# Stick-breaking attention, RG-LRU and squared-ReLU MLP on one core: value products in plain fp32 on the two halves of the array, one plan for the MLP and the front, a finer opening, aligned buffers

## The chip, the cores and the metric

The kernel runs on one core of one Trainium2 chip. The metric is the device time of one execution in microseconds (us), taken as the median of several runs. The core has five engines with their own instruction queues: PE (matmuls; its weight loads are listed apart as PEld), DVE, ACT, POOL, and SP, which here only issues DMAs. Everything is computed to fp32 accuracy.

## What is computed

One transformer-like block on x of 1024 tokens by 1024 channels; only the shapes and the products matter here:

```python
def hybrid_mixer(h, ...):                       # h = rms_norm(x): 1024 x 1024
    proj = h @ w_in                             # q, k, v of 512 each, xl and gl of 512 each
    q, k = rms_norm per head of 64              # 8 heads
    attn = stick_breaking_attention(q, k, v)    # per block of 128 queries:
        #   z = q k^T / 8 ; log_w = log_sigmoid(z) + suffix sums of log_sigmoid(-z)
        #   w = exp(log_w) below the diagonal, else 0 ; out = w @ v
    lru = rg_lru(conv(xl)) * gelu(gl)
    return concatenate([attn, lru]) @ w_out

x = x + hybrid_mixer(rms_norm(x))
x = x + square(relu(rms_norm(x) @ w_up)) @ w_down     # 1024 -> 4096 -> 1024
```

## The kernel before

**Precision.** A large product is made of three matmuls. Each operand is split into a high half (a copy that rounds to the type fp32r, made by ACT) and a low half (the source minus the high half, a two-input subtraction on DVE or POOL). PE then runs low by high, high by low and high by high into the same PSUM bank. A matmul of this kind has a 128x128 stationary operand and a moving operand of up to 512 columns. Operands of type plain F32 can be multiplied too, without a split.

**The front.** Everything up to the second norm is called the front. `record_front` writes it down as operations with an engine, a cost, the tiles read and the tiles written. `Plan.schedule` then makes a list schedule of these operations. The order in which units are considered is the table `ORDER`; `BIAS` shifts the due time of each kind of operation; `ALT` lists by number, unit by unit, which operations go to their other allowed engine (DVE instead of POOL and the like). Every instruction is issued in the order that the plan gives, so that in a trace all of the front carries the helper's line, L927.

- Opening: `iunit` (L481) loads, for eight channel chunks kc, a transposed piece of x (256 KB) and a piece of w_in (128 KB) alternately. ACT and DVE make `hTh` and `hTl` (128x512 halves of x) and the halves of `wq` (128x256). `chain` (L510) is the product of a weight column block with x: four steps of two chunks (six matmuls) each, so a step waits until two chunks are ready.
- `qunit`, `gunit`: queries, keys and their norms. `ss` is a plain fp32 product, four stationary operands of 128x32 next to each other in the array. `lunit`: the recurrent part; its `pg` is a plain fp32 product with a 64-row operand in each half of the rows.
- `vunit` (L583): values. ACT writes the high half, DVE the low half, so a head's stationary operand is 128 columns wide: 64 high and 64 low.
- `aunit` (L677): for a head pair p and a block c of 256 queries, scores `z`, sigmoids, scans, weights w. Then for every m from c down to 0 (256 keys) and each head h of the two, PE transposes four (or three, at m = c) 128x128 blocks of w into `pw`, ACT copies the high half to `wt`, DVE writes the low half, and PE runs four matmuls (two key blocks by high and low) of 128x256 into head h's half of `av`. At m = c one key block has only 128 columns. The high rows of `av` then hold the product of the high values, the other 64 rows that of the low values; ACT copies one out (`ot`) and DVE adds the other (`ob`), for each head. There are 80 such (p, c, m, h) groups.
- `ounit` (po): the product with w_out. `hunit` (ht): transposes of the result for the MLP.

**The MLP.** After the front's plan comes code that is written in a fixed order (line L1056 in traces). Two groups g of 2048 hidden channels are each computed with fewer, summed products in the manner of Strassen. A product is 12 matmuls of 128x512. A group has seven phases: 16, 24 and 16 products up (`p` in traces), then 16 (da, db), 16 (ea, eb), 16 (ga, gc) and 8 (ha) down (banks `pa`, `pb`, `pc`); 224 products in all. The sums of weights are POOL's or DVE's, the products' results in `U` are made by ACT, DVE and POOL, the high halves by ACT, and nearly all low halves by DVE (`split2`, L1068). The loop at L1354 runs the products in order and prepares the stationary operand of product q + 6 and the moving operand of q + 4 behind product q. Tiles come from rings of two pools each: 2 + 6 raw tiles, 2 + 4 stationary tiles, 8 + 4 moving tiles. The first number lies in pools on the left side of the memory, the second in pools on the right side. In each partition the left pools' tiles of the kernel before begin at a multiple of 256 bytes, the right pools' tiles 224 bytes above one.

Of the kernel before, what the change touches and what calls it, by code (L numbers as in the profile page):

```python
# [60 lines left out]

BIAS = {"vec": -30, "": 12, "x": 5, "hTh": -22, "hTl": 14, "wq": 5, "whq": -19, "wlq": 23, "ssx": 23, "wo": 15, "woh": -25, "wol": -18,
        "wv": 30, "whv": 4, "wlv": -30, "bd": -3, "pq": 19, "sq": 21, "qkl": 6, "pk": 8, "kf": -14, "ssq": -9, "sse": -22, "sst": 3,
        "var": 11, "pow": 17, "exp": 18, "rb": 15, "nrm": 1, "nrq": 17, "pv": 22, "vl": -16, "w_up": -13, "sth": -16, "stl": -19, "rsb": 14,
# [43 lines left out]
class Plan:  # L108
    def __init__(self):
        self.ops, self.queue, self.unit = [], {}, 0  # L110
        self.inunit, self.uname, self.flex = 0, "", []
        self.groups = {}

# [3 lines left out]
    def op(self, eng, cost, fn, r=(), w=(), set=None, grp=None, kb=0, what="", work=None, port=None, alt=None):  # L117
        o = Op()
        self.inunit += 1
# [81 lines left out]
    def schedule(self):  # L201
        free = {e: 0.0 for e in KEEP}
# [38 lines left out]
        while len(done) < n:  # L241
# [98 lines left out]
            for k in o.closes:  # L340
                left[k] -= 1
                late[k] = max(late[k], o.end)
                if not left[k]:
                    if not k:
                        q = self.queue["u"]
                        a = nxt["u"]
                        nxt["u"] = min(len(q), a + COUNT["uu"])
                        for i in range(a, nxt["u"]):
                            alloc(q[i], f"uu{i - a}", late[k] + 50)
                    for tag in OPENS[k]:  # L350
# [17 lines left out]
def record_front(plan, E, order):  # L368
# [75 lines left out]
    def xload(kc, ch):  # L444
        o = slice(512 * ch, 512 * ch + 512)
        xt = plan.tile("lg", f"xt{kc}{ch}")
        op("SP", 0, lambda kc=kc, xt=xt: E.sp.dma_start(xt[:, 0:512], E.xt[kc * P:(kc + 1) * P, o]), w=[xt], kb=256, what=f"x{kc}{ch}")
# [33 lines left out]
    def iunit():  # L481
        for kc in range(KC):
            xload(kc, 0)
            wload("q0", kc)
# [414 lines left out]
def kernel(ctx, tc, x, xt, vecs, w_in, w_rg, w_ig, w_out, w_up, w_down, out):  # L899
# [75 lines left out]
    for t in PTAGS:  # L975
        spools[t] = pool(psums, f"f_{t}", space=PSUM)
# [434 lines left out]
```

## Time and profile before

| | |
|---|---|
| median of 3 runs | 1107.29 us (1105.79 to 1111.71) |
| profiled execution | 1107.23 us, of which the span is 1105.3 us and 1.9 us lie around it |
| mean granted PE clock | 0.997 |
| DMA traffic | 120.82 MB, mean 109 GB/s |
| instructions | 15275, of them 5368 matmuls |

Times inside the profile count from the start of the span. A row of a group names line, engine, operation, output <- inputs, shapes and count, then the busy time and the mean ns of one, then the idle time of the engine just before these instructions and who ended it. A row of the timeline has start, duration, engine and form. The end of a matmul is modelled: matmuls overlap, so the time that one takes in a dense run is the distance between starts.

### The profile page before, as it was taken

What the parts mean: (1) busy time and instruction counts of PE and PEld (TensorE: products, weight loads), DVE (VectorE), ACT (ScalarE), POOL (GpSimd) and SP (SyncE); (2) the same over time, 40 slices, a digit from 0 to 9 for tenths busy, and PEclk for the clock granted to TensorE, in tenths of its full rate; (3) what the DMA queues carried; (4) which work ended last, traced back from release to release, by engine and by line L of the source; (5) the groups of instructions that cost most, each with busy time, mean ns of one, the idle gap of its engine ahead of it and who ended that gap; (6) DMA issues with size and microseconds to landing.
All of it is one profiled execution on the core that took longest, in us unless ns stands there. A gap on an engine that the chain in (4) does not pass through costs nothing.

```text
span 1105.3 us, 15275 instructions
## 1 busy us (share of the span) xinstructions
PE 1080.4 (98%) x5368; PEld 879.7 (80%) x5368; DVE 841.0 (76%) x1172; ACT 629.9 (57%) x1150; POOL 408.2 (37%) x340
## 2 busy tenths in 40 slices
PE   7999999999998999999999999999999999999998
PEld 5987778988777788777888888778887888888786
DVE  7498688848986886568557789987568676989964
ACT  7678689739986774446227843434554257543441
POOL 2420233022134211113443658734024425668431
PEclk9999999999999999999999999999999999999999
DMA  9311202111119101233333235555433332245654
GB/s 305 125 44 45 62 5 68 44 44 40 39 44 346 58 29 49 67 107 113 124 114 96 67 96 169 175 151 160 145 97 133 124 95 77 90 143 168 209 159 146
DMA packets 80636, 120.82 MB, mean 109 GB/s; under 512 B 9136, under 2 KB 29104, under 8 KB 80560
## 3 DMA queue, kind: packets, MB, share of 16 engines
q1 hardware_dynamic: 78256, 115.66, 33.3%
q10 hardware_dynamic: 2304, 4.20, 1.0%
q8 instruction: 42, 0.69, 0.3%
q14 instruction: 34, 0.28, 0.1%
HBM read 107.77 MB, written 12.06 MB: 108 GB/s over the span
## 4 chain that ended last, share of the span: by engine, by line
PE 85%; DVE 7%; ACT 4%; DMA 2%; issue 1%; SPq 0%; POOL 0%; DVEq 0%; ACTq 0%
PE p L1056 26%; PE pa L1056 16%; PE pb L1056 8%; PE po L927 7%; PE pq L927 5%; PE pv L927 4%; PE pc L1056 4%; PE pxl L927 3%; PE pgl L927 3%; PE av L927 3%; PE z L927 2%; PE pw L927 2%; DMA x<-in_xt_dram 1%; ACT x L927 1%; DVE h L927 1%
## 5 line engine op out<-in xcount | busy, mean ns | idle before, releaser
L1056 DVE TENSOR_TENSOR U<-p,U 128x512 f32<-128x512 f32 x80 | 55.1, 689 | 65.8 <-PE p L1056 65.7
L927 PE MATMUL pq<-hTh,wq 128*128 128x512 f32 x256 | 86.5, 404 | 8.0 <-DVE wq L927 6.4
L1056 PE MATMUL p<-m0t,st 128*128 128x512 f32 x384 | 92.0, 399 | 2.3 <-DVE U L1056 2.3
L1056 POOL TENSOR_TENSOR U<-U 128x512 f32<-128x512 f32 x48 | 68.1, 1426 | 67.5 <-ACT U L1056 32.9
L1056 PE MATMUL p<-m1t,st 128*128 128x512 f32 x384 | 90.1, 393 | 1.2 <-DVE U L1056 1.2
L1056 PEld LDWEIGHTS p<-m0t,st 128*128 128x128 f32 x384 | 73.1, 191 | 19.9 <-issue 2.7
L1056 PEld LDWEIGHTS p<-m1t,st 128*128 128x128 f32 x384 | 72.0, 188 | 18.0 <-ACT sb L1056 1.6
L927 DVE TENSOR_TENSOR wt<-pw,wt 128x512 fp32r<-128x512 f32 (+1 forms) x80 | 50.3, 629 | 26.9 <-ACT wt L927 26.5
L1056 PE MATMUL p<-m0b,sb 128*128 128x512 f32 x288 | 68.3, 394 | 1.7 <-DVE nrs L1347 1.7
L1056 PE MATMUL p<-m1b,sb 128*128 128x512 f32 x288 | 68.0, 393 | 0.0
L1056 POOL TENSOR_TENSOR r_sb<-r_sb,r_sa 128x512 f32<-128x512 f32 x16 | 22.9, 1429 | 116.4 <-DMA r_sb<-in_w_up_dram 55.2
L1056 PEld LDWEIGHTS p<-m0b,sb 128*128 128x128 f32 x288 | 53.9, 188 | 14.5 <-issue 1.9
L927 PEld LDWEIGHTS pq<-hTh,wq 128*128 128x128 f32 x256 | 49.2, 192 | 20.3 <-DVE wq L927 8.0
L1056 PEld LDWEIGHTS p<-m1b,sb 128*128 128x128 f32 x288 | 54.0, 188 | 12.5
L927 ACT CAST wt<-pw 128x512 fp32r<-128x512 f32 (+1 forms) x80 | 43.5, 543 | 35.9 <-PE pw L927 33.1
L927 POOL TENSOR_TENSOR w<-w,G 128x1024 f32<-128x1024 f32 (+3 forms) x18 | 31.4, 1747 | 87.0 <-ACT w L927 54.4
L1056 ACT ACTIVATE U<-U 128x512 f32<-128x512 f32 x96 | 58.9, 630 | 6.0 <-DVE U L1056 2.8
L927 ACT ACTIVATE G<-z,qv 128x512 f32<-128x512 f32 (+3 forms) x96 | 51.3, 586 | 14.1 <-PE z L927 8.7
L927 PE MATMUL av<-wt,v 128*128 128x256 f32 (+1 forms) x320 | 54.5, 295 | 3.3 <-DVE wt L927 2.4
L927 DVE TENSOR_TENSOR_SCAN G<-G,K 128x257 f32<-128x257 f32 (+3 forms) x32 | 48.3, 1531 | 9.6 <-ACT G L927 9.5
L927 PE MATMUL pq<-hTl,wq 128*128 128x512 f32 x128 | 50.9, 398 | 0.0
L927 ACT ACTIVATE w<-z,qv 128x512 f32<-128x512 f32 (+3 forms) x96 | 50.7, 604 | 0.1
(240 smaller groups left out, 2930.4 us busy)
## 6 DMA issues: line engine op xcount, KB each, us to landing
ro<-in_w_out_dram SPq DMA_DIRECT2D x20, 256.0 KB, 4.7
x<-in_xt_dram SPq DMA_DIRECT2D x16, 256.0 KB, 4.7
x<-in_x_dram SPq DMA_DIRECT2D x8, 512.0 KB, 5.6
wrl<-in_w_in_dram SPq DMA_DIRECT2D x32, 128.0 KB, 2.4
x<-in_x_dram SPq DMA_DIRECT2D x16, 256.0 KB, 5.7
r_a<-in_w_up_dram SPq DMA_DIRECT2D x16, 256.0 KB, 2.9
r_b<-in_w_up_dram SPq DMA_DIRECT2D x16, 256.0 KB, 2.8
r_sa<-in_w_up_dram SPq DMA_DIRECT2D x16, 256.0 KB, 3.3
```

The costliest lines, as they stand in the source:

```text
L927: self.last = tc.keep_in_program_order(getattr(self.eng, op)(*args, **kw))
L1056: ins = getattr(self.eng, op)(*args, **kw)
```

## The change

1. **Value products.** The values stay F32 (one copy, 64 columns per head) and so does `wt`: one copy per `pw` tile, allowed on ACT or DVE, and put on DVE for all 80 by `ALT`. Head h of a pair uses columns 64h to 64h + 63 of the array and writes partitions 64h to 64h + 63 of one `av` tile, the heads alternating. Two m's share one step on PE where there are two, so the 80 groups become 24. `ot` is gone; `ob` is one copy, or, where the result is used directly, nothing at all. PE has 160 matmuls in place of 320, in plain fp32.
2. **One plan.** `record_mlp` writes the MLP down as operations too, and the plan schedules front and MLP together. The low halves, sums and squares may go to POOL or DVE as `ALT` says. In all, POOL makes 179 of the MLP's low halves (3 before), and 38 of its weight sums (128 before). By the plan's units POOL has 12 to 18 two-input instructions in a phase of 16 products (15 and 14 in ea, eb of the first and second group), 35 and 28 in the phase of 24, and 15 in that of 8; DVE has 13 to 50 two-input instructions without PSUM in a phase of 16 (49 and 50 in ea, eb), 29 and 36 in that of 24, 15 and 9 in that of 8. The matmuls of neighbouring products, and of the last transposes of the front, may be interleaved. The stores of the sums `r2` move from ACT's queue to SP's (16 DMAs).
3. **Opening.** `chain` for the first weights goes in steps of one chunk (three matmuls), and `iunit` records the weight ahead of x.
4. **Alignment.** Pads (`align`, `falign`, K1 1056, lg 544) put the left pools' tiles at a multiple of 256 bytes and the right pools' tiles 128 bytes above one.

`ORDER`, `BIAS` and `ALT` are new tables throughout; the counts of tiles change with them (`A` 4 to 2, `wr` 7 to 3, `w` 9 to 16, `ob` 1 to 2).

DVE in the opening, before. `hTl` is the low half of a piece of x, `wq` that of a piece of w_in, the t_ and sp_ tiles are constants:

```order
L927 TENSOR_TENSOR hTl<-x_83,hTh 128x512
L927 SCALAR_TENSOR_TENSOR wq_196<-x_83,vec,wq_196 128x256
L927 TENSOR_SCALAR sp__104<-sp__104,t_c 128x4
L927 TENSOR_TENSOR hTl<-x_83,hTh 128x512
L927 SCALAR_TENSOR_TENSOR wq_205<-x_83,vec,wq_205 128x256
L927 TENSOR_TENSOR hTl<-x_83,hTh 128x512
L927 SCALAR_TENSOR_TENSOR wq_213<-x_83,vec,wq_213 128x256
```

The same place now:

```order
L1205 TENSOR_TENSOR hTl<-x_90,hTh 128x512 x4
L1205 SCALAR_TENSOR_TENSOR wq_205<-x_90,vec,wq_205 128x256
L1205 SCALAR_TENSOR_TENSOR wq_208<-x_90,vec,wq_208 128x256
L1205 SCALAR_TENSOR_TENSOR wq_212<-x_90,vec,wq_212 128x256
L1205 SCALAR_TENSOR_TENSOR wq_216<-x_90,vec,wq_216 128x256
L1205 SCALAR_TENSOR_TENSOR wq_219<-x_90,vec,wq_219 128x256
L1205 SCALAR_TENSOR_TENSOR wq_231<-x_90,vec,wq_231 128x256
L1205 TENSOR_TENSOR hTl<-x_90,hTh 128x512
L1205 SCALAR_TENSOR_TENSOR gcol<-vec 128x1
```

The first weight's low half now stands behind four pieces of x, and the weights follow each other. On SP five pieces of x and the small vectors are issued before the first piece of w_in, where x and w_in alternated before.

PE at a value product of the first pairs, before. `pw` are transposes of the weights w, `av` the value product, `pxl` a product of the recurrent part that fills in between:

```order
L927 MATMUL pxl_1130<-hTh,wl_875 128x512
L927 MATMUL pw_1152<-ident,w_946 128x128
L927 MATMUL pw_1152<-ident,w_964 128x128
L927 MATMUL pw_1152<-ident,w_946 128x128
L927 MATMUL pw_1152<-ident,w_964 128x128
L927 MATMUL av_1023<-wt_1137,v_734 128x256 x4
L927 MATMUL pxl_1130<-hTh,wl_879 128x512
```

The same engine now, where block c = 2 begins (`pg` is the recurrent part's gate product):

```order
L1205 MATMUL pg_1362<-x_90,bd 128x512
L1205 MATMUL pg_1363<-x_90,bd 128x512
L1205 MATMUL pw_1370<-ident,w_1296 128x128
L1205 MATMUL pw_1370<-ident,w_1308 128x128
L1205 MATMUL pw_1370<-ident,w_1296 128x128
L1205 MATMUL pw_1370<-ident,w_1308 128x128
L1205 MATMUL av_1376<-wt_1274,v_699 64x256 x2
L1205 MATMUL av_1376<-wt_1274,v_699 64x128 x2
L1205 MATMUL av_1376<-wt_1354,v_1035 64x256 x4
L1205 MATMUL pxl_1388<-hTh,wl_886 128x512
```

One step now holds both heads and two m's: eight fp32 matmuls on halves, in place of four groups of four on the whole width between other work.

PE where the front ends, before. `ht` are the last transposes, `p` the first products of the MLP:

```order
L927 MATMUL ht_5121<-ident,x_83 128x128 x8
L927 MATMUL ht_5131<-ident,x_83 128x128 x8
L927 MATMUL ht_5143<-ident,x_83 128x128 x8
L927 MATMUL ht_5155<-ident,x_83 128x128 x8
L1056 MATMUL p_00_5246<-m0b_4941,sb_4963 128x512 x3
L1056 MATMUL p_00_5246<-m0b_4949,sb_4963 128x512 x3
```

The same place now:

```order
L1205 MATMUL ht_4745<-ident,x_90 128x128 x8
L1205 MATMUL ht_4756<-ident,x_90 128x128 x8
L1205 MATMUL p_00_4776<-m0b_4645,sb_4603 128x512 x3
L1205 MATMUL ht_4799<-ident,x_90 128x128 x8
L1205 MATMUL ht_4815<-ident,x_90 128x128 x8
L1205 MATMUL p_00_4776<-m0b_4652,sb_4603 128x512 x3
```

Three matmuls of the MLP's first product now stand between the second and the third group of transposes.

The diff, cut to its core:

```diff
-SHAPE = dict(... wt=([2, 512], F32R), ob=([256], F32), ot=([256], F32), lg=([516], F32),
-             ... v=([4, 4, P], F32R), ... av=([2, 256], F32),
+SHAPE = dict(... wt=([2, 512], F32), ob=([256], F32), lg=([544], F32),
+             ... v=([4, 4, HD], F32), ... av=([256], F32),
+             ... bk=([512], F32), U=([8, 4, 512], F32))
+MORE = {2: (("mv", 4), ("st", 4), ("ra", 6)), 4: (("bk", 4),)}
...
+       "m71": (1, 2, 4, 6,), "m72": (4, 5, 6,), "m73": (1,), "m74": (4, 5, 6,), "m75": (1, 3,), "m76": (4, 5, 8, 10,), "m77": (1, 3, 5,), "m78": (4, 8,),
...
     def iunit():
         for kc in range(KC):
-            xload(kc, 0)
-            wload("q0", kc)
+            wload("q0", kc, "i")
+            xload(kc, 0, "i")
...
     def chain(pd, key, col, ch, name):
-        for g in range(4):
+        step = 1 if key == "q0" else 2
+        for g in range(0, KC, step):
             def mm(g=g):
-                for kc in (2 * g, 2 * g + 1):
+                for kc in range(g, g + step):
...
-            op("ACT", 482, lambda i=i, t=t, src=src: E.act.mul(vv[:, i, :, 0:HD], src(), E.rstd1[:, t:t + 1]),
-            op("DVE", 474, lambda i=i, t=t, src=src: E.dve.scalar_tensor_tensor(vv[:, i, :, HD:P], src(), E.rstd1[:, t:t + 1],
+            op("ACT", 482, ev, r=[pd, (rstd1, t // 2)], w=[(vv, i)], what=f"vh{pp}{t}", alt=("DVE", 430, False))
...
+        for g in range(c, -1, -2):
+            ms = [m for m in (g, g - 1) if m >= 0]
...
+                    def ev(e, ww=ww, pw=pw, nw=nw, h=h):
+                        (E.act.copy if e == "ACT" else E.dve.tensor_copy)(ww[:, h, :nw], pw[:, :nw])
...
-                        for x in (1, 0):
-                            E.pe.matmul(av[:, h, q0:256], VV[p // 2, t // 4][:, t % 4, 2 * (p % 2) + h, :], ww[:, x, 256 * jj:256 * jj + 256 - q0],
+                        for h in range(2):
+                            E.pe.matmul(av[HD * h:HD * h + HD, q0:256], VV[p // 2, t // 4][:, t % 4, 2 * (p % 2) + h, :], ww[:, h, 256 * jj:256 * jj + 256 - q0],
...
-            op("ACT", 367, lambda ot=ot, h=h, hs=hs, os=os: E.act.copy(ot[hs], av[os, h]), r=[(av, h)], w=[ot], what=f"ot{p}{c}")
-            op("DVE", 420, lambda ot=ot, h=h, hs=hs: E.dve.tensor_tensor(ob[hs], av[hs, h], ot[hs], op=ALU.add), r=[(av, h), ot], w=[(ob, h)], what=f"ob{p}{c}")
+        op("ACT", 380, lambda e: (E.act.copy if e == "ACT" else E.dve.tensor_copy)(ob[:], av[:]), r=[av], w=[ob], what=f"ob{p}{c}", alt=("DVE", 420, False))
...
+def record_mlp(plan, E, base):
...
+    def split(tag, name, src, what):
+        v = plan.tile(tag, name)
+        op("ACT", 626, lambda: E.act.copy(v[:, 0], src[1]()), r=[src[0]], w=[(v, 0)], what=f"{what}h")
+
+        def low(e):
+            on(e).tensor_tensor(v[:, 1], src[1](), v[:, 0].bitcast(F32), op=ALU.subtract)
+        op("DVE", 687, low, r=[src[0], (v, 0)], w=[(v, 1)], what=f"{what}l", port=True, alt=("POOL", 1285, True))
+        return v
...
+            if store:
+                R2[g, k] = V(plan, None, f"r2{g}{k}")
+                op("SP", 0, lambda: E.sp.dma_start(E.r2[g][k], raw[:]), r=[raw], w=[R2[g, k]], kb=256, what="rst")
...
+    pool(ctx, "align", side="right").tile([P, 24], F32, name="align")
...
-                return lgs[:, 516 * v.slot:516 * v.slot + 516]
+                return lgs[:, 544 * v.slot:544 * v.slot + 544]
...
     record_front(plan, E, ORDER)
+    record_mlp(plan, E, len(ORDER))
     plan.schedule()
```

More of the change, by code (lines that the diff above doesn't have):

```diff
@@ L349, in schedule @@
                             alloc(q[i], f"uu{i - a}", late[k] + 50)
+                    for tag, more in MORE.get(k, ()):
+                        q = self.queue.get(tag, [])
+                        b = min(COUNT[tag], len(q))
+                        nxt[tag] = max(nxt.get(tag, 0), b)
+                        for i in range(nxt[tag], min(len(q), nxt[tag] + more)):
+                            alloc(q[i], COUNT[tag] + i - nxt[tag], late[k] + 50)
+                        nxt[tag] = min(len(q), nxt[tag] + more)
                     for tag in OPENS[k]:
@@ L518, in mm @@
                     E.pe.matmul(pd[:], w[:, 0, s], E.hTh[:, kc, m], start=False, stop=kc == KC - 1)
-            r = [(hT, (x, kc, ch)) for x in "hl" for kc in (2 * g, 2 * g + 1)]
-            op("PE", 6 * 228, mm, r=r + [W[key][2 * g][0], W[key][2 * g + 1][0]], w=[pd], what=name)
+            r = [(hT, (x, kc, ch)) for x in "hl" for kc in range(g, g + step)]
+            op("PE", 3 * step * 228, mm, r=r + [W[key][kc][0] for kc in range(g, g + step)], w=[pd], what=("i" if step == 1 else "") + name)
     SQ, RQ = {}, {}
@@ L945 @@
     nc.vector.memset(E.mhalf, -0.5)
-    E.rs2, E.w_out = rs2, w_out
+    E.rs2, E.w_out, E.w_down, E.out = rs2, w_out, w_down, out
+    E.nrs2 = const.tile([P, NT], F32, name="nrs2")
+    E.r2 = [dram.tile([8, P, 512], F32, name=f"r2_{g}") for g in range(2)]
     psums, left, right, late = ExitStack(), ExitStack(), ExitStack(), ExitStack()
@@ L973 @@
     nc.vector.memset(E.K1[:, 512:513], 1.0)
-    for t in PTAGS:
-        spools[t] = pool(psums, f"f_{t}", space=PSUM)
+    psz = ExitStack()
+    spools["z"] = pool(psz, "f_z", space=PSUM, side="left")
+    for t in CLOSES[3]:
+        spools[t] = pool(psums, f"f_{t}", space=PSUM, side="right")
     for t in CLOSES[1]:
@@ L979, with openu @@
     spools["wr"] = pool(right, "f_wr", side="right")
-    class Ring:
-        def __init__(self, na, nb):
-            self.na, self.n, self.i, self.pools = na, na + nb, 0, [None, None]
-        def tile(self, shape, dtype, **kw):
-            self.i += 1
-            return self.pools[(self.i - 1) % self.n >= self.na].tile(shape, dtype, **kw)
-    rwr, stp, mvp = Ring(2, 6), Ring(2, 4), Ring(8, 4)
-    rings = {"ra": (rwr, "r", 2), "st": (stp, "t", 2), "mv": (mvp, "t", 8)}
+    def openu():
+        if "U" not in spools:
+            late.close()
+            spools["U"] = pool(ctx, "units", side="right")
+            for t, _ in MORE[2]:
+                spools[f"{t}_"] = pool(ctx, f"{t}_", side="right")
     class Maker(Plan):
@@ L1005, in make @@
                     left.close()
-                    spools["h2"] = pool(ctx, "h2")
-                    for t, (ring, _, n) in rings.items():
-                        ring.pools[0] = pool(ctx, t, bufs=n)
-                if v.tag in rings:
-                    return rings[v.tag][0].tile([P] + shape, dt, tag=rings[v.tag][1], name=v.name)
+                    for t in OPENS[1]:
+                        spools[t] = pool(ctx, t)
+                if v.slot >= COUNT[v.tag]:
+                    openu()
+                    return spools[f"{v.tag}_"].tile([P] + shape, dt, tag=slot, name=v.name)
+            if v.tag == "U":
+                openu()
+            if v.tag == "bk":
+                k = v.slot >= COUNT["bk"]
+                if ("bk", k) not in spools:
+                    (psz if k else psums).close()
+                    spools["bk", k] = pool(ctx, f"bk{int(k)}", space=PSUM, side="left" if k else "right")
+                return spools["bk", k].tile([P] + shape, dt, tag=slot, name=v.name)
             if v.tag == "x1":
@@ L1330, in moving @@
-    def moving(n):
-        nonlocal free
-        if n < len(PR) and PR[n].mov is not None:
-            PR[n].item.add()
-            PR[n].mov()
-            free += PR[n].free
-    for k in ("0b11", "0b21"):
-        movs[k] = {u: (E.first[k, u][:, 0], E.first[k, u][:, 1]) for u in range(4)}
-    for n in range(2):
-        PR[n].st = E.first["st", n][:, 0], E.first["st", n][:, 1]
-        ITEMS[n].raws, ITEMS[n].at, ITEMS[n].summed = [], -NSTAT, True
-    nload, pinned = 2, True
-    U = pool(ctx, "units", side="right").tile([P, 8, 4, 512], F32, name="U")
@@ L1345 @@
-    for pl, nm, n in ((mvp, "mb", 4), (stp, "sb", 4), (rwr, "rb", 6)):
-        pl.pools[1] = pool(ctx, nm, bufs=n, side="right")
-    nc.vector.tensor_scalar_mul(nrs2, rs2, -1.0)
-    limit, free = len(ITEMS), free + 6
-    load_items(-NSTAT)
-    for n in range(2, NSTAT):
-        stat(n)
-        low()
-        load_items(-NSTAT)
-    for q, pr in enumerate(PR):
-        pr.mm()
-        for fn in pr.early:
-            fn()
-        if pr.early:
-            low()
-        stat(q + NSTAT)
-        moving(q + MAHEAD)
-        pr.ev()
-        if not pr.hold:
-            low()
-        for fn in pr.after:
-            fn()
-        if not pr.hold:
-            low()
-        load_items(q)
-        if q + UAHEAD < len(PR) and PR[q + UAHEAD].usum is not None:
-            PR[q + UAHEAD].usum()
-        for it in ITEMS[:nload]:
-            if it.at <= q - WLAG:
-                it.add()
```

576 lines of the change are left out of this document (271 added, 305 removed), and 56 rows, old and new, of tables (ALT, BIAS, ORDER).

## The prediction

> **What bounds the kernel now.** I read the page first: the span, the busy times and the chain that ended last.
>
> ```profile
> span 1105.3 us, 15275 instructions
> PE 1080.4 (98%) x5368; PEld 879.7 (80%) x5368; DVE 841.0 (76%) x1172; ACT 629.9 (57%) x1150; POOL 408.2 (37%) x340
> PE 85%; DVE 7%; ACT 4%; DMA 2%; issue 1%; SPq 0%; POOL 0%; DVEq 0%; ACTq 0%
> ```
>
> PE is busy 98% of the span and makes 85% of the chain. So time can come from three places only: PE's idle 24.9 us (1105.3 - 1080.4), matmuls that take longer than they need, and work that PE no longer does. The table by stretches says where the idle time lies. Its columns are the stretch, its length, then busy time and count of PE, PEld, DVE, ACT and POOL, the granted clock, the DMA share and GB/s.
>
> ```profile
> 0.00:24.00 24.00, 17.17 (x60) 12.71 (x60) 17.49 (x53) 17.66 (x33) 6.14 (x19) 1.00 0.93 293
> 24.00:300.00 276.00, 273.82 (x1703) 227.99 (x1704) 208.33 (x332) 213.87 (x415) 64.23 (x94) 1.00 0.18 56
> 300.00:400.00 100.00, 95.84 (x542) 77.19 (x542) 82.51 (x116) 71.20 (x135) 31.38 (x35) 0.98 0.36 127
> 400.00:471.00 71.00, 68.03 (x380) 57.24 (x378) 48.87 (x72) 35.48 (x66) 15.37 (x9) 1.00 0.18 56
> 471.00:524.00 53.00, 50.53 (x218) 40.82 (x219) 38.26 (x52) 29.99 (x54) 12.25 (x8) 1.00 0.38 115
> 631.00:720.00 89.00, 89.00 (x385) 71.76 (x384) 82.86 (x85) 38.11 (x67) 64.41 (x37) 1.00 0.47 145
> 720.00:840.00 120.00, 117.67 (x507) 94.59 (x506) 87.08 (x121) 60.62 (x108) 32.22 (x22) 1.00 0.44 136
> 1034.00:1105.00 71.00, 67.32 (x290) 53.83 (x288) 47.35 (x66) 22.84 (x40) 22.87 (x14) 1.00 0.51 167
> ```
>
> Length less PE's busy time gives the idle time: 6.8 us in the opening, 2.2 + 4.2 + 3.0 = 9.3 us in the rest of the front (to 471), 2.5 and 2.3 us in the MLP, 3.7 us at the end. From 631 to 720 there is none. The table of waits says who was late: DVE's small operands in the opening and at the value products, and DVE's results `U` in the MLP.
>
> ```profile
> PE pq L927 <- DVE wq L927: 6.4, 2, 5.8
> PE p L1056 <- DVE U L1056: 3.4, 2, 2.3
> PE av L927 <- DVE wt L927: 2.4, 2, 1.5
> PE pw L927 <- DVE wt L927: 1.3, 2, 0.9
> ```
>
> The sum is made against the profiled execution, 1107.2 us (span 1105.3 and 1.9 around it), which is the median of the runs shown (1107.3) within 0.1 us. About 0.5%, 5.5 us, is what a measurement of this kernel can tell from no change.
>
> **Alignment, -9 us.** Every MLP product is 12 equal matmuls with nothing late, yet in the chain of waits they don't take equally long:
>
> ```profile
> 945.13 2.75 PE pa L1056 x12
> 947.88 2.73 PE pb L1056 x12
> 950.61 2.80 PE pa L1056 x12
> 953.41 2.80 PE pb L1056 x12
> ...
> 978.48 2.75 PE pa L1056 x12
> ```
>
> ```profile
> 471.19 38.99 PE p L1056 x168
> ```
>
> From 945.13 to 978.48 stand twelve products in 33.35 us. Four take 2.74 on average, eight 2.80; the rows repeat with a period of twelve, as the rings of 6 and 12 tiles do. The four fast ones are those whose stationary and moving tiles lie on the same side of the memory, so at the same offset modulo 256 bytes; the slow ones mix 0 and 224. At 2.74 for all, twelve products would take 32.9, 0.45 less, so 112 down products give 4.2 us. In the up phases 14 products take 38.99, 2.785 each; 0.045 less over 112 gives 5.0. Together 9 us, if offsets 0 and 128 count as alike. No row shows that pair, so the bounds are 0 and -9.4. I take -9, since in all rows the duration goes by how the two offsets stand to each other and not by the side itself (fast on the left, fast on the right).
>
> **Value products, -4 us.** The rows for the cost of before, and the two nearest to the new form, plain fp32 matmuls on parts of the array (`ss`: four quarters of the columns; `pg`: two halves of the rows, with score products z running between):
>
> ```profile
> 110.71 0.72 PE L927 MATMUL av<-wt,v 128*128 128x256 f32 x4
> 111.26 0.40 PE L927 MATMUL pq<-hTh,wq 128*128 128x512 f32 x1
> 133.17 1.07 PE L927 MATMUL ss<-sq,ones 128*32 128x512 f32 x8
> 134.17 0.50 PE L927 MATMUL pxl<-hTh,wl 128*128 128x512 f32 x1
> 144.29 1.22 PE L927 MATMUL pg<-x,bd 64*128 64x512 f32 x3
> 145.35 0.59 PE L927 MATMUL pg<-x,bd 64*128 64x512 f32 x1
> ```
>
> Before: a group of four takes 111.26 - 110.71 = 0.55 us. There are 48 of these and 32 with two narrower matmuls, between 0.41 (three quarters) and 0.55, taken as 0.43: 26.4 + 13.8 = 40 us (39.5 to 44). After: `ss` ran four matmuls of 512 columns, recorded as eight passes, in 134.17 - 133.17 = 1.00 us. So one round of passes side by side takes 0.50 for 512 columns, entry and exit included, hence 0.25 for 256. An m below c needs four rounds for both heads (two key blocks, two passes): 1.00 us, 24 times; m = c needs 0.75, 16 times: 36 us. That is -4. Below: 0.45 a round for 512 columns (four times a matmul of 2.74 / 12 = 0.228, two passes) gives 33 us, -8 at most against 40. Above: `pg`, where the two halves were not in step; the fourth pass starts 1.06 after the first and lasts about 0.5 more, 1.55 for what `ss` does in 1.00. That makes 56 us, +16. I take the `ss` row, as it splits columns, as the change does.
>
> Each step also changes how the array is divided, 24 times. In `ss` entry and exit are within the 1.00 us, so they cost at most 0.10 of it, 2.4 us over 24 steps, and are in the sum. The Trainium skill, "TensorEngine Tiling (Array Packing)", section "Key Properties", speaks against the change here: switching the tiling mode drains TensorE. If a drain cost what a matmul row outlasts its turn, 0.40 - 0.23 = 0.17 at entry and exit, 24 steps would cost 8 us and the term would be about +2 instead of -4; the `ss` row shows less.
>
> **Value products off PE.** These rows carry the wait between transposes and value products:
>
> ```profile
> L927 ACT CAST wt<-pw 128x512 fp32r<-128x512 f32 x48 | 28.1, 586 | 31.0 <-PE pw L927 29.9 <-PE av L927 1.1
> L927 DVE TENSOR_TENSOR wt<-pw,wt 128x512 fp32r<-128x512 f32 x48 | 32.7, 682 | 21.3 <-ACT wt L927 21.2
> ```
>
> Before, `pw` passes through ACT (0.59) and then DVE (0.68) before `av`. Now one copy on DVE, priced as the subtraction, 0.68: the way is shorter by 0.59 a group, and DVE's 21.2 us of waiting for ACT goes. ACT loses 80 casts and 32 `ot`, DVE 32 additions; neither is the bound, so their time itself counts nothing.
>
> **Front stalls and seam, -5.5 us.** The waits for `wt` above, 2.4 + 1.3 = 3.7 us, should go with the shorter way. Of the 3.0 us idle before 471, where PE first waits for the last transposes' inputs and then for the MLP's first operands, the three MLP matmuls between the transposes and the planned order should cover about 1.8. What is late next: `av` steps hold two m's and so wait for four copies; with 2 `A` tiles in place of 4, scores wait for DVE and POOL earlier. Behind such an `av` stand fill-in matmuls that could have run. Bounds: -9 (all idle gone) to +5 (half as much again).
>
> **Opening, +1 us.**
>
> ```profile
> 5.83 0.80 PE L927 MATMUL pq<-hTh,wq 128*128 128x512 f32 x1 [5.83 <-DVE wq L927]
> 6.43 0.63 PE L927 MATMUL pq<-hTl,wq 128*128 128x512 f32 x1
> 6.85 0.63 PE L927 MATMUL pq<-hTh,wq 128*128 128x512 f32 x1
> 8.95 0.62 ACT L927 CAST hTh<-x 128x512 fp32r<-128x512 f32 x1 [0.16 <-DMA x<-in_xt_dram]
> 12.70 0.40 PE L927 MATMUL pq<-hTl,wq 128*128 128x512 f32 x1
> 24.08 0.50 PE L927 MATMUL pq<-hTh,wq 128*128 128x512 f32 x1 [0.54 <-ACT sq L927]
> ```
>
> 60 matmuls by 24 us need 13.7 at 0.228; 10.3 us are lost. PE starts at 5.83, at first with 0.42 from start to start (6.43 to 6.85), with the full pace from about 12.7; 13 matmuls start till then. The fourth piece of x is there at 8.95, after about 1.4 to 1.5 MB of alternating pieces. The new order has five pieces of x (1.25 MB) before the first of w_in, so that one lands at 8.3 to 9 as well; with 0.5 each on ACT and DVE the first matmul comes at about 9.7, 4 us later. But then PE needs just one more weight piece (128 KB, 0.44 us at 293 GB/s) per three matmuls and stays dense. If it is slow for 3 to 6.9 us from there, it loses 9.7 + 0.46 x 3 to 6.9 = 11.1 to 12.9; the wait of 0.54 at 24.08 and its like go. So +1 (-1 to +3). The x pieces issued ahead delay nothing but these weights.
>
> **MLP stalls, -1.5 us.** Of 2.5 + 2.3 us idle, a plan that may run three matmuls of another product should save a part; -4.8 to +5. The 16 stores that move from ACT's queue to SP's (among its loads) each wait for a sum; behind one stands the next load, with six to eight raw tiles in reserve: nothing. The end of the kernel keeps its chain of evacuation and store: nothing.
>
> Sum: -9 - 4 - 5.5 + 1 - 1.5 = -19; 1107.2 - 19 = 1088 us.
>
> **Rivals.**
>
> *0 and 128 are not alike.* Then the first term is lost: 1097 us. For it: mixed offsets are slow in every row where they occur. Chance 0.13.
>
> *Halves not in step.* By the `pg` rows +16 in place of -4: 1108 us, no change; wholly one after the other, 72 us, +32: 1124. It decides for slower when a round of both heads passes 0.42 us for 256 columns (60 us in all). Against it: `ss`. Chance 0.09, of that 0.03 for serial.
>
> *Low halves on POOL come late, slower.* The rows, alone and beside each other:
>
> ```profile
> L927 DVE TENSOR_TENSOR f<-f,rb 128x512 f32<-128x512 f32 x8 | 5.5, 684 | 2.9 <-PE rb L927 2.9
> L927 POOL TENSOR_TENSOR k<-f,k 128x512 fp32r<-128x512 f32 x4 | 5.1, 1286 | 2.8 <-ACT k L927 2.8
> L1056 POOL TENSOR_TENSOR r_sb<-r_sb,r_sa 128x512 f32<-128x512 f32 x16 | 22.9, 1429 | 116.4 <-DMA r_sb<-in_w_up_dram 55.2
> L1056 POOL TENSOR_TENSOR r_ea<-r_ea,r_ec 128x512 f32<-128x512 f32 x16 | 35.1, 2192 | 1.3
> ```
>
> The same operation on POOL takes 1.29 us alone and up to 2.19 beside a busy DVE. If DVE and POOL took turns, ea/eb would need 15 x 1.286 + 49 x 0.684 = 52.8 us, against 16 x 2.74 = 43.8 of PE, and ha 15 x (1.286 + 0.684) = 29.6 against 21.9; the second group 52.2 and 25.4. The overshoots, 9.0 + 7.7 + 8.4 + 3.5 = 29 us, would be PE's wait: 1117 us. It decides in ha first, where a mean over 1.46 us (21.9 / 15) on POOL is too long; 1429 is just under. Against taking turns: from 631 to 720, 85 DVE and 37 POOL instructions need 85 x 0.684 + 37 x 1.286 = 105.7 us by themselves (94.8 if 16 of DVE's read PSUM), ran in 89.00, and PE did not wait. The Trainium skill, "SBUF — State Buffer", section "SBUF: two separate sides", calls the shared port an exclusive lock against which the loser fully blocks; by that rule this rival would hold, and the stretch just named goes against it. Chance 0.09, of that 0.08 slower.
>
> *The change does not do what it says.* The tiles still meet at unlike offsets and the new order only moves the waits: -4 + 1 leaves 1104, no change. Chance 0.07.
>
> **How the numbers follow.** Forecast 0.62, with its own range from 1075 (all terms at their low ends) to 1101. Faster: forecast and first rival, 0.75. Same: 0.06 + 0.01 + 0.07 = 0.14. Slower: 0.03 + 0.08 = 0.11. A range to 1108 takes in the first rival, the `pg` case and the last rival and leaves out 0.03 + 0.09 and some of the forecast's lower end: 1075 to 1108.
>
> **What would show it.** Right: all MLP products at 2.73 to 2.75 in the chain, `av` steps of 1.5 to 2 us for eight matmuls, DVE's `wt` copies without waits for ACT, PE's idle time in 24 to 471 under 5 us, a first matmul near 9.7. Wrong: products at 2.80 still, or at another mix; `av` rows that take over 3 us for eight matmuls; waits of PE for POOL's low halves in ha and ea/eb; PE's idle time above 25 us.

## The result and the profile after

The changed kernel takes 1093.38 us (median of four runs, 1092.76 to 1094.39), the kernel before 1109.3 us on the same chip (1105.79 to 1111.71): a ratio of 0.987, with a 95% interval of 0.984 to 0.990. The profiled executions differ by 13.5 us (spans 1105.3 and 1091.8), and it is this difference that is taken apart below.

The page of the changed kernel, span, busy times and chain:

```profile
span 1091.8 us, 15111 instructions
PE 1070.5 (98%) x5368; PEld 856.4 (78%) x5368; DVE 812.3 (74%) x1095; ACT 574.9 (53%) x1023; POOL 461.6 (42%) x396
PE 92%; DVE 3%; DMA 2%; ACT 2%; issue 1%; SPq 0%; DVEq 0%; ACTq 0%
```

PE's busy time fell by 9.9 us, its idle time from 24.9 to 21.3. The table by stretches (stretch, length, busy time and count of PE, PEld, DVE, ACT and POOL, clock, DMA share, GB/s) shows where:

```profile
0.00:24.00 24.00, 14.07 (x53) 11.42 (x54) 16.11 (x44) 16.44 (x32) 4.89 (x16) 1.00 0.90 285
24.00:300.00 276.00, 270.75 (x1685) 214.04 (x1683) 211.66 (x340) 178.30 (x319) 58.39 (x83) 1.00 0.19 58
300.00:400.00 100.00, 98.46 (x567) 74.03 (x565) 76.48 (x105) 60.94 (x111) 25.90 (x37) 1.00 0.41 139
400.00:467.00 67.00, 66.35 (x385) 52.39 (x384) 44.48 (x64) 29.27 (x55) 15.94 (x16) 1.00 0.10 33
467.00:520.00 53.00, 53.00 (x233) 43.28 (x232) 31.95 (x38) 25.70 (x48) 38.46 (x28) 1.00 0.39 115
620.00:720.00 100.00, 100.00 (x434) 81.35 (x434) 86.17 (x105) 46.42 (x82) 45.12 (x31) 1.00 0.48 144
1010.00:1092.00 82.00, 77.86 (x337) 62.98 (x336) 56.34 (x63) 26.68 (x46) 41.69 (x28) 1.00 0.51 159
```

The opening lost ground: 9.9 us idle instead of 6.8, 53 matmuls instead of 60. The rest of the front has 5.3 + 1.5 + 0.7 = 7.4 us of idle time instead of 9.3. The MLP has none before its end. The table of waits agrees: the waits of av for wt and of the MLP for `U` are gone, pw's wait for wt stayed. A row gives the total wait, how often, and the longest.

```profile
PE pq L1205 <- DVE wq L1205: 9.9, 1, 9.9
PE pw L1205 <- DVE wt L1205: 2.1, 2, 1.1
PE pq L1205 <- DVE q L1205: 1.6, 1, 1.6
PE po L1205 <- DVE mxl L1205: 1.5, 1, 1.5
```

In the chain, whole MLP products still take unequal times, from 2.72 to 2.81:

```profile
750.70 24.99 PE pa L1205 x108
...
987.47 2.79 PE pa L1205 x12
...
995.09 2.72 PE pb L1205 x12
```

Matched with the addresses of their tiles, the 1548 MLP matmuls on unlike offsets (0 with 128) take 0.2323 us from start to start, the 1135 on alike ones 0.2294; before, 0.2333 (0 with 224) and 0.2284. A value step of eight matmuls in the timeline:

```profile
104.59 1.95 PE L1205 MATMUL av<-wt,v 128*64 128x256 f32 x16
106.47 0.50 PE L1205 MATMUL pgl<-hTh,wl 128*128 128x512 f32 x1
```

It takes 106.47 - 104.59 = 1.88 us for two m's and two heads. Summed from start to start over the 320 records of each trace, without PE's idle time, the value products take 43.9 us before and 35.0 after.

Divided at the fourth matmul of the MLP (471.96 us before, 467.08 after) and at the last one (1101.05 and 1087.47), the 13.5 us are 4.9 in the front and 8.7 in the MLP; the end is alike.

### The profile page after: what moved, and what is told of

It is laid out like the page before. It is cut to its first block, busy times and chain, and to the rows that moved or that the text cites. A ratio compares the mean times of both kernels' runs of the same rounds, so it can differ in the third digit from the quotient of the medians.

```text
span 1091.8 us, 15111 instructions
## 1 busy us (share of the span) xinstructions
PE 1070.5 (98%) x5368; PEld 856.4 (78%) x5368; DVE 812.3 (74%) x1095; ACT 574.9 (53%) x1023; POOL 461.6 (42%) x396
## 4 chain that ended last, share of the span: by engine, by line
PE 92%; DVE 3%; DMA 2%; ACT 2%; issue 1%; SPq 0%; DVEq 0%; ACTq 0%
PE p L1205 28%; PE pa L1205 16%; PE pb L1205 8%; PE po L1205 8%; PE pq L1205 6%; PE pv L1205 4%; PE pc L1205 4%; PE pxl L1205 4%; PE pgl L1205 3%; PE z L1205 3%; PE pw L1205 3%; PE av L1205 3%; DMA x<-in_x_dram 1%; ACT x L1205 1%; PE pg L1205 1%
## 5 line engine op out<-in xcount | busy, mean ns | idle before, releaser
L1205 DVE COPY wt<-pw 128x512 f32<-128x512 f32 (+1 forms) x80 | 50.3, 629 | 28.7 <-PE pw L1205 26.6
L1205 ACT ACTIVATE w<-z,qv 128x512 f32<-128x512 f32 (+3 forms) x96 | 48.2, 592 | 16.6 <-PE pw L1205 16.5
L1205 DVE TENSOR_TENSOR_SCAN G<-G,K 128x769 f32<-128x769 f32 (+3 forms) x32 | 48.3, 1522 | 6.0 <-ACT G L1205 6.0
L1205 PE MATMUL pv<-wv,hTh 128*128 128x256 f32 x256 | 49.5, 287 | 0.0
L1205 PE MATMUL po<-woh,mxl 128*128 128x512 f32 x112 | 46.9, 419 | 1.5 <-DVE mxl L1205 1.5
L1205 PEld LDWEIGHTS pw<-ident,w 128*128 128x128 f32 x288 | 34.0, 140 | 18.0 <-DVE wt L1205 5.9
L1205 POOL MEMSET G<- 128x1 f32 x64 | 4.1, 98 | 103.5 <-DVE w L1205 59.9
L1205 PE MATMUL pw<-ident,w 128*128 128x128 f32 x288 | 45.6, 276 | 2.1 <-DVE wt L1205 2.1
```

The costliest lines, as they stand in the source:

```text
L1205: self.last = tc.keep_in_program_order(getattr(self.eng, op)(*args, **kw))
```

## The experiments

Every kernel is compared with runs of the kernel before on its own chip: 1108.4 us beside m1_pairs, e1_right0, e3_values and e4_open_alt, 1107.9 beside e5 to e8, 1107.0 beside e9 and e10. Where matmul work "by" a time is given, it is the sum over the matmuls started till then, each at its time in a dense run.

**Which operands are alike.** One kernel with matmuls alone, on chosen places, and with the value products' two forms.

```diff
+PAIRS = (("ca", 0, 16384), ("cb", 0, 16392), ("cc", 0, 16400), ("cd", 0, 16416), ("ce", 0, 16424), ("cf", 0, 16432), ("cg", 0, 16440),
+         ("ch", 0, 16448), ("ci", 0, 16512), ("cj", 0, 16640), ("ck", 0, 16896), ("cl", 0, 17152), ("cm", 56, 16440), ("cn", 32, 16416),
+         ("co", 0, 2048), ("cp", 0, 34816), ("cq", 34816, 0), ("cr", 34848, 0), ("cs", 34872, 0), ("ct", 34872, 16440))
```

> This kernel leaves the whole computation out: it runs 60 matmuls of 128x512 in the MLP's pattern (low by high, high by low, high by high; four stationary blocks of 128 columns) for each of 20 pairs of places of the moving and the stationary operand in one large tile that begins at a multiple of 4096 bytes, and then three series of 16 for the value products. Theory one (offsets): a matmul is slow when its two operands stand at different offsets modulo some power of two, wherever they lie. Then pairs at equal offsets, near or far, take 0.227 us per matmul, 13.6 to 13.7 us for 60, and pairs at unlike offsets 0.232 to 0.234, 13.9 to 14.0 us; which of the distances 32, 64, 96, 128, 160, 192, 224, 256, 512, 1024, 2048, 3072 bytes are slow gives the power of two. Theory two (sides): offsets do not matter, and pairs that lie far from each other in the memory are slow at any offset. Then all pairs at one distance of 64 KB take alike, and the pair at 8 KB is faster than those at 136 KB, or all take 0.227. For the value products: 16 fp32 matmuls of 64x256 in alternate halves of the columns take 3.6 to 4.1 us if the halves run side by side (eight rounds of two passes at 0.225 to 0.25), and as long as the series in one half, 7.2 us, if not.

The timeline of this kernel; a pair's time is the distance to the next start. The numbers of a pair are the places of the moving and of the stationary operand in floats (cd: 128 bytes from alike, ce 160, cf 192, cg 224, ch 256, cn both at 128, cp alike 136 KB apart, cr moving at 128 and stationary at 0 and far). A distance of 96, which the expectation lists, was not run:

```profile
53.03 14.11 PE L26 MATMUL cd<-big 128*128 128x512 f32 x60
66.98 14.15 PE L26 MATMUL ce<-big 128*128 128x512 f32 x60
80.97 13.89 PE L26 MATMUL cf<-big 128*128 128x512 f32 x60
94.70 14.16 PE L26 MATMUL cg<-big 128*128 128x512 f32 x60
108.70 13.76 PE L26 MATMUL ch<-big 128*128 128x512 f32 x60
122.30 13.76 PE L26 MATMUL ci<-big 128*128 128x512 f32 x60
...
190.34 13.81 PE L26 MATMUL cn<-big 128*128 128x512 f32 x60
203.99 13.77 PE L26 MATMUL co<-big 128*128 128x512 f32 x60
217.59 13.76 PE L26 MATMUL cp<-big 128*128 128x512 f32 x60
231.19 13.76 PE L26 MATMUL cq<-big 128*128 128x512 f32 x60
244.79 14.15 PE L26 MATMUL cr<-big 128*128 128x512 f32 x60
258.78 14.15 PE L26 MATMUL cs<-big 128*128 128x512 f32 x60
...
286.47 3.67 PE L26 MATMUL va<-src 128*64 128x256 f32 x32
289.97 7.07 PE L26 MATMUL vb<-src 128*64 128x256 f32 x32
296.97 2.17 PE L26 MATMUL vc<-big 128*128 128x256 f32 x16
```

Theory one holds: 13.60 us for 60 (0.227 each) when the two offsets are equal modulo 256 bytes (ch, ci, co, cp, cq), whatever the distance, 13.65 with both at 128 (cn); 13.95 to 14.00 (0.233) when they are not, 128 among them (cd, cr). Of the distances run, only 192 (cf) has a partial cost, 13.73. How far apart the operands lie does not matter. The value products in two halves take 3.50 us (va), a little under the 3.6 to 4.1 expected, in one half 7.00 (vb): the halves run side by side.

**Right tiles at multiples of 256 bytes.** In the changed kernel:

```diff
-    pool(ctx, "align", side="right").tile([P, 24], F32, name="align")
+    pool(ctx, "align", side="right").tile([P, 56], F32, name="align")
```

> The changed kernel with the right side's pad 56 instead of 24 floats wide, so that left and right tiles all begin at a multiple of 256 bytes. Theory one (the offsets of the two operands must be equal modulo 256, and 0 with 128 is as bad as 0 with 224): the MLP's mixed matmuls go from 0.2323 to about 0.229 us as the others, 1540 of them by 3.3 ns, so 5 us less in all, 1088, and products in the chain of waits at 2.72 to 2.76. Theory two (left with right is slow at any offset): nothing moves, 1092 to 1095, products at 2.80 as before.

Measured 1081.06 us (1080.63 to 1081.40), ratio to before 0.976 (0.974 to 0.978), 12.3 below the changed kernel. The chain:

```profile
744.12 24.48 PE pa L1205 x108
...
973.64 2.72 PE pb L1205 x12
976.36 2.72 PE pa L1205 x12
```

All MLP matmuls take 0.2267 us. Theory one is right in its direction and short in its size: it expected 5 us, from the unlike matmuls alone, but the alike ones went from 0.2294 to 0.2267 as well. Why the alike ones were slow too stays open. Unlike neighbours are not all of it: in the trace of the kernel before, the ten alike products with alike ones on both sides take 0.2280 per matmul as well.

**The same pad in the kernel before.**

```diff
+    pool(ctx, "align", side="right").tile([P, 56], F32, name="align")
     E.x1 = pool(ctx, "x1", side="right").tile([P, NT, D], F32, name="x1")
```

> The kernel before with nothing but a pad of 56 floats on the right side, so that all its tiles begin at a multiple of 256 bytes. Theory (the distance of the two operands modulo 256 bytes alone sets the pace): 1600 mixed MLP matmuls go from 0.2333 to 0.227 us, 10 us less, 1096 to 1100, and the chain's products all take 2.72 to 2.76. Rival (the gain needs the interleaved order of the new plan): 1102 to 1106.

Measured 1096.45 us (ratio 0.990, 0.988 to 0.992), 11.4 less than before beside it. The products:

```profile
937.03 2.72 PE pa L1057 x12
939.75 2.72 PE pb L1057 x12
```

So alignment by itself is worth what was forecast for it and a little more, and does not need the new order; it only has to be modulo 256 bytes.

**The value products alone.** The kernel before with the new `vunit` and `aunit` tails, every copy on DVE, old tables:

```diff
-            op("ACT", 482, lambda i=i, t=t, src=src: E.act.mul(vv[:, i, :, 0:HD], src(), E.rstd1[:, t:t + 1]),
+                    E.act.mul(vv[:, i], src(), E.rstd1[:, t:t + 1])
...
+        for g in range(c, -1, -2):
+            ms = [m for m in (g, g - 1) if m >= 0]
...
+                    op("DVE", 165 + 1.02 * nw, lambda ev=ev: ev("DVE"), r=[pw], w=[(ww, h)], what=f"wth{p}{c}")
...
+                            E.pe.matmul(av[HD * h:HD * h + HD, q0:256], VV[p // 2, t // 4][:, t % 4, 2 * (p % 2) + h, :], ww[:, h, 256 * jj:256 * jj + 256 - q0],
```

> The kernel before with the new value products alone: values and weights in plain fp32, two heads in the halves of the columns, two key blocks' pairs in a step, one copy on DVE; tables, opening, MLP and addresses' pads as before. Theory: the value products take 35 us in place of 44 whatever stands around them, and the waits for wt shrink, so -9 to -12 us, 1096 to 1100. Rival: the old tables are tuned for the old steps, and new waits for four copies at a time eat the gain: 1103 to 1110.

Measured 1112.43 us (ratio 1.006, 1.003 to 1.008). The value products do take 35.0 us, 8.9 less, but the kernel is slower: the rival is right, and a little low. Waits of PE that are new or longer (pw's was 1.3):

```profile
PE pw L930 <- DVE wt L930: 2.6, 2, 2.1
PE po L930 <- DVE x L930: 2.4, 2, 2.0
```

Between first and last matmul PE idles 19.8 us instead of 15.2, pw takes 3.7 us more and pg 2.9 more from start to start, without idle time. Two attempts at which feature of the new steps does this:

```diff
-                    op("DVE", 165 + 1.02 * nw, lambda ev=ev: ev("DVE"), r=[pw], w=[(ww, h)], what=f"wth{p}{c}")
+                    op("ACT" if h else "DVE", (170 + .815 * nw) if h else (165 + 1.02 * nw), lambda ev=ev, h=h: ev("ACT" if h else "DVE"), r=[pw], w=[(ww, h)], what=f"wth{p}{c}")
```

> The kernel before with the new value products, as in e3_values, but the copy of head 1's transposes on ACT and only that of head 0 on DVE. The values alone lost 4 us although the value products themselves fell from 43.9 to 35.0 us of PE. Theory: the loss is the queue on DVE, where every copy stands behind scans and other copies while PE waits for the single pw buffer; with half of the copies on ACT, which has 54 us less to do than before, the transposes and their neighbours wait less: 1100 to 1107. Rival: the loss is that a step of two m's waits for four copies and then holds PE for a whole run, wherever the copies are made; then it stays at 1110 to 1114.

Measured 1126.17 us (ratio 1.016, 1.014 to 1.018): neither; it lost 14 us more.

```diff
-        for g in range(c, -1, -2):
-            ms = [m for m in (g, g - 1) if m >= 0]
+        for g in range(c, -1, -1):
+            ms = [g]
```

> The kernel before with the new value products, as in e3_values (1112.4 us), but one m per step of PE as before instead of two, so that a step waits for two copies and not for four. Theory: the wait of a step for four copies and its long hold of PE is what ate the saving; then PE's idle time falls from 19.8 to 15 to 17 us and the time is 1098 to 1106. Rival: it is the old tables' order as a whole, which was tuned for other durations; a planner with other steps gives another order, not a better one, and the time stays at 1108 to 1116.

Measured 1134.71 us (ratio 1.024, 1.021 to 1.027). The theory falls here too, and the rival's range was too low as well: PE's idle time is 32.2 us, of which one wait, far from any value step, has 12.4:

```profile
373.99 0.76 PE L930 MATMUL po<-woh,mxl 128*128 128x512 f32 x1 [12.37 <-DVE x L930]
```

Each of the three gives the planner other durations, and it writes another order of the whole front from tables that were made for the old ones: of the front's 2072 records on PE outside pw and av, 428 to 499 are of another tile than the record at the same place in the trace of before. The value products themselves take 35.0, 34.9 and 38.0 us in the three, all less than before, so what is lost lies elsewhere. That the order is what loses it is argued, not shown: no run puts the new value products into the old order by exchange.

**The fine steps of the opening alone**, in the kernel before:

```diff
-        for g in range(4):
+        step = 1 if key == "q0" else 2
+        for g in range(0, KC, step):
```

> The kernel before with the first weights' chain in steps of one chunk, the loads alternating as before. Theory: PE starts at about 5.5 us and has done 0.3 to 1 us more work by 24 us (more than 13.65 us of matmuls), and if the rest of the order is as good, the time is 1106 to 1108. Rival: any change of steps makes the planner give another order for the whole front, and its waits outweigh the start: 1110 to 1120, with more idle time of PE after 32 us.

Measured 1116.37 us (ratio 1.009, 1.006 to 1.011). The start gained 0.2 us, a little less than the theory had (13.88 us of matmuls by 24 us instead of 13.65), and by 40 us it was 3.9 us behind (25.80 instead of 29.73): the rival.

**The order of the opening's loads.** In the changed kernel, first by the planner's numbers, of which two change:

```diff
-BIAS = {"vec": -11, "": 27, "x": -9, "hTh": 11, "hTl": 10, "wo": 18, "woh": 3, "wol": 9, "iwq": -14, "iwhq": -25, "iwlq": -30, "ix": -23,
+BIAS = {"vec": -30, "": 27, "x": -9, "hTh": 11, "hTl": 10, "wo": 18, "woh": 3, "wol": 9, "iwq": -23, "iwhq": -25, "iwlq": -30, "ix": -23,
```

> The changed kernel with vec first and w_in and x alternating again in the opening's loads (three numbers of BIAS), the steps of one chunk kept. Theory one: five pieces of x ahead of the first weight cost the start: the first matmul comes at 5.5 to 6.5 us instead of 9.9, by 24 us there are 58 to 62 matmuls instead of 53, and the time is 1.5 to 3 us lower. Rival: what arrives by 24 us is bounded by the DMA's rate, PE starts earlier and waits more: the same number of matmuls by 30 us and the same time, 1092 to 1095.

Measured 1102.06 us (ratio 0.994, 0.993 to 0.996), 8.7 above the changed kernel. The start came nearly as foreseen, with the first matmul at 5.1 and 57 matmuls by 24 us, but again the whole plan had moved and PE idled 8 us more. So the same was done without a new plan, by exchanging these operations alone in the finished order (in e1_right0's kernel):

```diff
     plan.schedule()
+    first = lambda o: o.unit == ORDER.index("I") or o.what == "vec"
...
+    for e in ("SP", "ACT", "DVE"):
+        at = [i for i, o in enumerate(seq[e]) if first(o)]
+        for i, o in zip(at, sorted((seq[e][i] for i in at), key=lambda o: -1 if o.what == "vec" else o.prio[1])):
+            seq[e][i] = o
```

> The kernel of e1_right0 (the change with right tiles at multiples of 256 bytes, 1081.1 us) with vec first and w_in and x alternating in the queues of SP, ACT and DVE for the first weights alone; the order of everything else stays as planned, which it did not in e4_open_alt. Theory one: five pieces of x first cost 2 to 3 us, so 1078 to 1079.5, first matmul at 5 to 6. Rival: what counts comes later, the waits at 25 to 32 us for DVE's later steps, and nothing is won: 1080.5 to 1082.

Measured 1080.57 us (1080.32 to 1080.79), 0.5 below e1_right0: the rival. Against the kernel before on their own chips both stand at 0.976, so 0.5 us is no clear gain. First the timeline of the changed kernel, then of e1_right0, then of this one, at their first matmul and at the last wait of the opening:

```profile
9.93 0.79 PE L1205 MATMUL pq<-hTh,wq 128*128 128x512 f32 x1 [9.93 <-DVE wq L1205]
...
26.86 0.50 PE L1205 MATMUL pq<-hTh,wq 128*128 128x512 f32 x1 [1.58 <-DVE q L1205]
```

```profile
9.50 0.79 PE L1205 MATMUL pq<-hTh,wq 128*128 128x512 f32 x1 [9.50 <-DVE wq L1205]
...
25.70 0.50 PE L1205 MATMUL pq<-hTh,wq 128*128 128x512 f32 x1 [0.44 <-DVE q L1205]
```

```profile
5.40 0.80 PE L1205 MATMUL pq<-hTh,wq 128*128 128x512 f32 x1 [5.40 <-ACT hTh L1205]
...
25.30 0.50 PE L1205 MATMUL pq<-hTh,wq 128*128 128x512 f32 x1 [0.99 <-DVE q L1205]
```

It starts 4.1 us earlier than e1_right0 and waits at nearly the same place for the same data, and longer: by 32 us it has done 19.57 us of matmuls, e1_right0 19.34. The two are the fastest of the kernels that compute the block (this one's ratio to before has an interval of 0.974 to 0.977), ahead of both kernels of the study.

**The low halves back on DVE.** The changed kernel without ALT's entries for the MLP, all but one; the sums of weights go back to POOL with them:

```diff
...
-       "m71": (1, 2, 4, 6,), "m72": (4, 5, 6,), "m73": (1,), "m74": (4, 5, 6,), "m75": (1, 3,), "m76": (4, 5, 8, 10,), "m77": (1, 3, 5,), "m78": (4, 8,),
...
```

> The changed kernel without ALT's entries for the MLP: the low halves go back to DVE and the sums to POOL, as in the kernel before, but still in one plan; the front's order is the same. Theory one (POOL's low halves took away the MLP's stalls): PE idles again for 3 to 10 us in the MLP and the time is 1096 to 1104. Theory two (the common order did it, and DVE has room): the MLP stays as long, 620 us from its fourth to its last matmul, and the time is 1092 to 1095.

Measured 1121.39 us (ratio 1.013, 1.011 to 1.015). The MLP takes 650.9 us from its fourth to its last matmul instead of 620.4. Of PE's 19.5 us of idle time there, 15.2 lie where da and db run, in both groups, and most of the rest at the start of ea and eb (the rows of the stretches, the largest wait, and DVE's row for the operand waited for):

```profile
620.00:720.00 100.00, 89.02 (x360) 70.17 (x360) 73.69 (x90) 41.40 (x74) 51.96 (x37) 0.95 0.47 155
...
920.00:1010.00 90.00, 82.18 (x336) 64.76 (x335) 68.87 (x81) 45.18 (x81) 55.27 (x39) 0.96 0.46 149
```

```profile
PE pb L1183 <- DVE sdb L1183: 12.2, 7, 3.1
```

```profile
L1183 DVE TENSOR_TENSOR sdb<-U,sdb 128x512 fp32r<-128x512 f32 x16 | 21.9, 1367 | 0.0
```

DVE comes to these halves late and without a pause before them. Some 7 of the other 11 us that the MLP lost are slow matmuls: behind each of the five waits of 2.4 to 3.6 us, five to eight matmuls start 0.43 apart instead of 0.23. Theory one, and by more than it expected. The changed kernel's one plan runs the MLP without a wait, with the low halves and sums shared out; without the shares it waits 19.5 us; the fixed order of before, with nearly all low halves on DVE, waited 4.7. So it seems to be the two together, the list order and the shares that its table was made with; no run has the shares in the old fixed order.

## Why the prediction came out as it did

The time, 1093.4, lies in the range and the direction is right, but the forecast of 1088 stood on terms that failed in both directions. That the sum came as near as it did is partly luck: alignment and the front's stalls were forecast too large by 12 us together, the value products and the MLP's stalls too small by 11.5.

- **Alignment, -9: failed.** The step that failed is "I take -9", with its reason that the rows go by how the offsets stand to each other. That is so, but nothing in the rows said that 0 and 128 stand alike. The first rival came true for this term: unlike matmuls went from 0.2333 to 0.2323, 0.6 us summed over the MLP's dense matmuls. Modulo 256 (e1_right0, e7_before_right0) the term measures 11 to 12.
- **Value products, -4: mis-sized.** They gave 8.9. The new form was priced well (36, measured 35.0), the old one not: 40, with 0.55 a group and 0.43 a narrower one. Groups that stand alone take 0.58 and 0.51 on average, and the sum, 43.9, is the upper end of the bounds given. The halves run side by side (va against vb), so the second rival is out. The change of the array's division is small: eight matmuls took 1.88 us with entry and exit; their eight rounds of passes at va's pace (3.50 / 16 = 0.22) are 1.75, which leaves 0.13. Steps of one full m take 1.015, so two of them 0.15 more than the one step of 1.88, by the trace of the changed kernel. Both stay below the 0.34 that the reading of the Trainium skill ("TensorEngine Tiling (Array Packing)", "Key Properties") as a full drain would have given.
- **The way from pw to av.** DVE's wait for ACT and av's wait for wt are gone, as forecast; pw's wait for wt is not (1.3 before, 2.1 now).
- **Front stalls, -5.5: too much.** The idle time of 24 us to the end of the front fell by 1.9: from 3.0 to 0.7 at the seam, where 1.8 was forecast to go, from 4.2 to 1.5 in 300 to 400, but it rose from 2.2 to 5.3 before 300, 1.58 of it a wait of the first weights' chain at 26.86. In addition the other front matmuls run somewhat less dense (pw 2.3 us more, pgl 1.6, po 1.5, z 2.5 less), from start to start; the reason stays open. The value products alone are a loss (e3_values); their 8.9 us become a gain only with tables made for them.
- **Opening, +1: at its upper end.** First matmul at 9.93 (9.7 forecast), 53 matmuls by 24 us (7 short, 1.6 us of work), and PE idle for 9.9 us instead of 6.8, 3.1 more. The wait of 1.58 just behind, which the sum did not have, is in the front's idle time above; in e1_right0, with the same opening, it was 0.44. The reason was only half right: loads in the old order start PE 4.1 us earlier than in e1_right0 and win 0.5 at most (e8_open_only).
- **MLP stalls, -1.5: too little.** The idle 4.8 us went wholly, and so did some 3 us of matmuls that start late without idle time, six at 0.43 apart behind the wait of 2.3 us among them: with the 0.6 of alignment the MLP is 8.7 us shorter. The lower bound was -4.8, because only idle time was counted.
- **Low halves on POOL: no, but not for the reason given.** In ha POOL takes 1.41 us for them, just under the 1.46 from which ha was to be late, and PE waits nowhere in the MLP:

```profile
L1205 POOL TENSOR_TENSOR sha<-U,sha 128x512 fp32r<-128x512 f32 x11 | 15.5, 1413 | 4.0 <-ACT sha L1205 4.0
```

Nor did these halves cost time: the kernel that gives them and the sums back is 28 us slower (e6_lows_dve). But the argument against taking turns was misread. It added up 0.684 and 1.286 us, which is how long an instruction lasts; alone, DVE's next instruction starts 0.60 after and POOL's 1.25 after. The timeline of the kernel before, of POOL and then of DVE, shows the turns in the very stretch that was to rule them out:

```profile
679.17 6.49 POOL L1056 TENSOR_TENSOR r_ea<-r_ea,r_ec 128x512 f32<-128x512 f32 x1
...
690.73 1.75 POOL L1056 TENSOR_TENSOR U<-U 128x512 f32<-128x512 f32 x1
692.44 1.74 POOL L1056 TENSOR_TENSOR r_ea<-r_ea,r_eb 128x512 f32<-128x512 f32 x1
```

```profile
681.43 0.68 DVE L1056 TENSOR_TENSOR sea<-U,sea 128x512 fp32r<-128x512 f32 x1
682.03 0.68 DVE L1056 TENSOR_TENSOR mea<-r_ea,mea 128x512 fp32r<-128x512 f32 x1
...
691.25 1.78 DVE L1056 TENSOR_TENSOR meb<-r_ec,meb 128x512 fp32r<-128x512 f32 x1
692.95 1.78 DVE L1056 TENSOR_TENSOR sea<-U,sea 128x512 fp32r<-128x512 f32 x1
```

From 679.02 on DVE runs nine two-input instructions 0.60 apart, and one sum on POOL lasts 6.49 us. Then the two alternate, one instruction of each per 1.70 us. This agrees with the exclusive lock of the Trainium skill ("SBUF — State Buffer", "SBUF: two separate sides"). By starts, 631 to 720 needs 74 x 0.60 + 37 x 1.25 = 91 us, or 85 with the 1.70 - 0.60 = 1.10 that POOL takes in such a pair (11 of the 85 DVE instructions read PSUM): taking turns about fits in 89.00. In the changed kernel, between 620 and 720 us, 85 such DVE instructions and 31 of POOL's need 90 us by the same count and ran in 100 with PE never idle. So, as far as these sums go, the rival failed on its prices and not on the turns. Its ha would still need 15 x 1.70 = 25.5 us against 21.9; in the one plan, ha's products lie among those of ga and gc (753 to 776 within 710 to 777), and PE did not wait.

What the terms measured: alignment -0.6, value products -8.9, front stalls -1.9, opening +3.1 and MLP -8.1, with 2.9 for the less dense front, make -13.5.

## What to carry to other kernels

When equal matmuls take two durations in the chain, look at the addresses of both operands: equal offsets modulo 256 bytes cost one pad and gave 1% here, and a pair of offsets that no row shows is worth a rival, not a term. Where a planner with tuned tables writes the order, a part of a change must not be judged by planning it anew with tables made for something else: the value products, the fine steps and the load order each made the kernel slower so, though each did on its own place nearly what it should. To price one edit, exchange operations in the finished order instead. And when two engines are said to share or to take turns, count from start to start: durations of neighbours overlap.

## What the runs showed of the hardware

- A matmul of 128x512 takes 0.227 us when its moving and stationary operands stand at equal offsets modulo 256 bytes and 0.233 at the other distances run (0.229 at 192), however far apart they lie.
- Plain fp32 matmuls in the two halves of the columns overlap fully: 16 of 64x256 in 3.50 us in alternate halves, 7.00 us in one half.
- A matmul step in two column halves between full-width matmuls costs 0.13 to 0.15 us over its own passes, entry and exit together.
- DVE and POOL take turns at two-input work from SBUF (128x512): DVE alone starts every 0.60 us, POOL alone every 1.25; side by side, one of each takes 1.70 us, and one sum on POOL lasted 6.49 us beside nine instructions of DVE.
- Behind a wait of PE of 2.4 to 3.6 us in the MLP, five to eight matmuls started 0.43 us apart instead of 0.23 (e6_lows_dve).
